# Held value products in the first attention, and an opening that loads tokens and weights in turn

## The chip, the cores and the metric

The kernel runs on one NeuronCore of one Trainium2 chip. The metric is the device time of one execution in microseconds (us). TensorE multiplies matrices, VectorE (DVE) and ScalarE (ACT) work element by element, GpSimd (POOL) does a few small powers, and the queue of SyncE (SP) issues all the DMA transfers. Each engine takes its instructions in the order in which they stand in its own stream.

## What is computed

The reference is two transformer blocks on one sequence of 512 tokens of width 1024, all in float32. The change touches the first block alone, whose first half is this:

```python
h = rms_norm(x, norm_pre)
proj = h @ w_in
(q_n, k_c, v_c, k_s, v_s, k_w, v_w, g_n, z_n, ...) = split(proj)
# 8 query heads of 64, 2 groups of keys and values; gates g_n per head and branch
o_a = compressed attention + selected attention + window attention, each gated
y_a = (o_a * silu(z_n)) @ w_nsa_o
```

With 512 tokens the selected branch and the window branch are both plain causal softmax attention, over keys k_s, k_w and values v_s, v_w. The compressed branch attends to 31 summaries of the keys and values. Behind it the block has a retention, two gates and an output projection; the second block has two feed-forward layers, a mixer with a second attention and a state-space part, and a cross attention.

## The kernel before, in words

Tokens lie in four tiles of 128 (t from 0 to 3). **Projections** multiply float32 numbers split in two float32r parts, a high and a low one, with three products each (high by high, low by high, high by low): `proj_T` (line 143, products at line 164) and `proj_X` (line 194, products at line 209). `wload` (line 102) loads a chunk of weights of 128x1024 by one DMA (line 99, three buffers `raw`), and `split` (lines 82 and 83) makes the high part on ACT and the low part on DVE, in two buffers each of `whi` and `wlo`. `proj_X` goes over the chunks of weights (four of them for a depth of 1024) and multiplies each with all four token tiles; only for the last `tail` chunks it goes token tile by token tile, so that a tile can be consumed when it is done.

**The opening** (lines 309 to 319) issues the DMA of token tile 0, of the constants `cst` (with the identity for transposes) and of the gain, then of the other three token tiles. Each tile is normalised (`prenorm_tile`, line 242: a sum of squares on ACT at line 249, the power on POOL at line 76, the scaling on DVE at line 251), turned by eight float32 transposes on TensorE (line 236) and split into `a_hi` and `a_lo`. The first projection (line 402, keys and values of 512 columns) then asks for its weights.

**The first attention** (`attention`, line 485) takes one token tile of queries (`qi`) at a time. It begins with the compressed branch: scores at line 495, a softmax on DVE and ACT, two transposes at line 510, and eight value products at line 516 into the bank `ob`. Then come eight steps, two branches times four pairs of heads. A step has float32r score products (line 536), the mask and minimum on DVE (line 539), the exponential on ACT (line 541), small factors on DVE (lines 542 to 544), the scaling of the two heads on DVE (line 546), float32 transposes of the probabilities on TensorE (line 553, one for each head and key tile), copies of these out of PSUM on ACT and DVE (lines 556 and 558), and float32 value products (line 561, one for each head and key tile, 64 columns of weights each, two records in the trace for one product). `qi` has qi+1 key tiles. When all is in `ob`, `gated` (line 565) multiplies it with `zn` on DVE.

The float32 products (transposes and values) and the float32r products (scores and projections) share TensorE. The order in the engine streams is not the program's order: a planner places, by its own estimate of times, the earliest instruction in program order that is ready. So scores of later steps and products of the projections that follow in the program (`zn`, then the rotated queries and keys of the retention, all at line 164) are placed wherever a step of the attention waits. The second attention, in the mixer, has a form of its own: `after` (line 88) adds a dependence, the transposes of a step (line 1055) wait for the last DVE operation of that step (line 1048), and the value products (line 991) of the step before are held back and follow those transposes.

Of the kernel before, what the change touches and what calls it, by code (L numbers as in the profile page):

```python
# [7 lines left out]
F32 = mybir.dt.float32  # L8
F32R = mybir.dt.float32r
AF = mybir.ActivationFunctionType  # L10
ALU = mybir.AluOpType
# [20 lines left out]
def block_kernel(ctx, tc, A, out, upto=99):  # L32
# [69 lines left out]
    def wload(src, k0, nk, c0, w, slot=None):  # L102
        raw, _ = wraw(src, k0, nk, c0, w)
        n = nk * w
        hi, lo = slot() if slot else (wp.tile([128, 1024], F32R, name="whi"), wp.tile([128, 1024], F32R, name="wlo"))
        split(hi[:, :n], lo[:, :n], raw[:, :n])
        return (hi[:, :n].rearrange("p (k c) -> p k c", k=nk), lo[:, :n].rearrange("p (k c) -> p k c", k=nk))
# [85 lines left out]

    def proj_X(src, c0, w, get, consume, K=8, nt=NT, tail=1, kp=2, korder=None, between=None, slots=()):

# [21 lines left out]
        slots = (None,) * (tail - len(slots)) + tuple(slots)  # L217
        last = [(ch, wload(src, ko[ch * kp], min(kp, K - ch * kp), c0, w, slots[ch - nch])) for ch in range(nch - tail, nch)]
        for t in range(nt):
# [81 lines left out]
    def first_block():  # L301
# [7 lines left out]
        x0 = xp.tile([128, NT, D], F32, name="x_in", tag="x")  # L309
        for t in range(NT):  # L310
            nc.sync.dma_start(x0[:, t], x2d[:, t])
            if t == 0:
                nc.sync.dma_start(cst, A["c_a"])
                g0 = gain("norm_pre")
            if t == 0:
                pair = new_act()
            if t == 0:
                hs = l1.tile([128, NT, D], F32, name="hs", tag="s3")
            prenorm_tile(x0[:, t], g0, pair, t, halved(hs[:, t]))
        get = act_get(pair)  # L320
        cb_t = cb.tile([128, B_ALL], F32, name="cb_t")
# [9 lines left out]
        bcast(A["b_nsa_gate"], 24, bg)  # L331
        w_in = A["w_in"]

# [67 lines left out]

        proj_X(w_in, 512, 512, get, ev_kv)
        proj_X(w_in, 1024, 280, get, ev_kw)
# [74 lines left out]

        ns = [0]

# [4 lines left out]
        def attention(qi):  # L485
            ob = op_.tile([128, 512], F32, name="ob").rearrange("p (a q) -> p a q", a=4)
            qsl = slice(qi * 128, (qi + 1) * 128)
# [18 lines left out]
            V.scalar_tensor_tensor(c8, c8, valid[:, qi:qi + 1], gv[:, 0], op0=ALU.mult, op1=ALU.mult)  # L506
            V.tensor_tensor(pc, pc, c8[:, :, None].to_broadcast([128, 8, 32]), op=ALU.mult)
            tp = tpp.tile([128, 4, 128], F32, name="tp")
            for g in range(2):
                PE.transpose(tp[:, g], pc[:, g * 4:(g + 1) * 4].rearrange("p a b -> p (a b)"), ident)  # L510
            pT = l2.tile([128, 2, 128], F32, name="pTc", bufs=1)
            V.tensor_copy(pT, tp[:, 0:2])
            for a in range(4):
                for e in range(2):
                    h = 2 * a + e
                    PE.matmul(ob[64 * e:64 * e + 64, a], vcD[:, h // 4, h % 4], pT[:, h // 4], start=(a == 0), stop=False,
                              skip_group_check=True)

            nk = qi + 1
            W = nk * 128  # L520
            for br in range(2):
                for a in range(4):
# [22 lines left out]
                    for e in range(2):  # L545
                        V.tensor_scalar(p[:, e, :W], p[:, e, :W], c2[:, e:e + 1], None, op0=ALU.mult)
                    tp = None
                    for e in range(2):
                        if e == 0 or nk > 2:
                            tp = tpp.tile([128, 4, 128], F32, name="tp") if (e if nk > 2 else a % 2) else bank((2,)).rearrange("p (j q) -> p j q", j=4)  # L550
                            o = 0
                        for j in range(nk):
                            PE.transpose(tp[:, o + j], p[:, e, j * 128:(j + 1) * 128], ident)  # L553
                        o += nk
                        if nk > 2:
                            (V.tensor_copy if e else ACT.copy)(pT[:, e, :nk], tp[:, :nk])
                    if nk <= 2:
                        (V.tensor_copy if a % 2 else ACT.copy)(pT[:, :, :nk], tp[:, :2 * nk].rearrange("p (e j) q -> p e j q", e=2))
                    for j in range(nk):
                        for e in range(2):  # L560
                            PE.matmul(ob[64 * e:64 * e + 64, a], vv[:, j, br, g * 64:(g + 1) * 64], pT[:, e, j], start=False,  # L561
                                      stop=(br == 1 and j == nk - 1), skip_group_check=True)
            return ob

        def gated(qi, ob):
            V.tensor_tensor(zn[:, :, qi * 128:(qi + 1) * 128], zn[:, :, qi * 128:(qi + 1) * 128], ob, op=ALU.mult)

# [4 lines left out]

        ob = attention(0)
        proj_T(w_in, 1304, 512, get, ev_zn, of=(0, 1))
        gated(0, ob)
        for qi in range(1, NT):
            gated(qi, attention(qi))

# [689 lines left out]
```

## Time and profile before

| | us |
|---|---|
| median of three runs | 1963.53 |
| lowest and highest of them | 1960.84, 1966.74 |
| the profiled execution, its own time | 1966.04 |
| its span in the trace | 1964.3 |
| TensorE busy in the span | 1907.7 |

The profile is of one execution. Its page gives busy time by engine, the chain of work that ended last, and groups of instructions by line. The trace behind it can be asked for the instructions in order of time (a timeline, in which neighbours of one kind are merged), for groups by line within a stretch, for the busy time of every engine in given stretches, and for waits (which engine waited before which line, for whom, how long and how often). A busy TensorE is an upper bound of its work, because the ends of products are modelled: the start of one product and the start of the next say more than their durations.

### The profile page before, as it was taken

What the parts mean: (1) busy time and instruction counts of PE and PEld (TensorE: products, weight loads), DVE (VectorE), ACT (ScalarE), POOL (GpSimd) and SP (SyncE); (2) the same over time, 40 slices, a digit from 0 to 9 for tenths busy, and PEclk for the clock granted to TensorE, in tenths of its full rate; (3) what the DMA queues carried; (4) which work ended last, traced back from release to release, by engine and by line L of the source; (5) the groups of instructions that cost most, each with busy time, mean ns of one, the idle gap of its engine ahead of it and who ended that gap; (6) DMA issues with size and microseconds to landing.
All of it is one profiled execution on the core that took longest, in us unless ns stands there. A gap on an engine that the chain in (4) does not pass through costs nothing.

```text
span 1964.3 us, 24168 instructions
## 1 busy us (share of the span) xinstructions
PE 1907.7 (97%) x9676; PEld 1555.6 (79%) x9676; DVE 1002.7 (51%) x1712; ACT 709.0 (36%) x1190; POOL 38.0 (2%) x66
## 2 busy tenths in 40 slices
PE   7999999999999999999999999989999999999998
PEld 5677788788878888888877777667788888888887
DVE  5578743824563333323668666785464553333223
ACT  4345433223242222223445433344353432323221
POOL 0000000100000000000000000000000000000000
PEclk9999999999999999999999999999999999999999
DMA  7411033232323333234231255542262322333332
GB/s 243 119 55 33 23 87 97 74 118 87 97 95 97 98 98 97 97 97 129 74 96 43 76 135 124 130 127 67 84 192 87 97 65 86 97 97 97 97 97 86
DMA packets 153560, 191.10 MB, mean 97 GB/s; under 512 B 9732, under 2 KB 111464, under 8 KB 153320
## 3 DMA queue, kind: packets, MB, share of 16 engines
q1 hardware_dynamic: 153448, 189.56, 32.1%
q8 instruction: 76, 1.25, 0.3%
q14 instruction: 36, 0.29, 0.0%
HBM read 174.85 MB, written 2.10 MB: 90 GB/s over the span
## 4 chain that ended last, share of the span: by engine, by line
PE 80%; DVE 10%; ACT 2%; DMA 1%; issue 1%; POOL 1%; SPq 0%; POOLq 0%; DVEq 0%; ACTq 0%
PE mm L164 40%; PE mm L209 27%; PE mm L187 3%; DVE E L1045 2%; PE ob L561 1%; POOL rp_r L76 1%; DVE x_sb L279 1%; DVE l L1048 1%; DVE h L251 1%; DVE wlo L83 1%; PE ob L902 1%; PE s L536 1%; PE s L1143 1%; DVE fg L272 1%; PE mm L553 1%
## 5 line engine op out<-in xcount | busy, mean ns | idle before, releaser
L83 DVE TENSOR_TENSOR wlo<-raw,whi 128x1024 fp32r<-128x1024 f32 (+1 forms) x276 | 336.1, 1218 | 681.4 <-ACT whi L82 676.0
L82 ACT ACTIVATE whi<-raw 128x1024 fp32r<-128x1024 f32 (+1 forms) x276 | 291.1, 1055 | 698.5 <-PE mm L164 298.5
L164 PE MATMUL mm<-a_hi,wlo 128*128 128x512 f32 x1120 | 439.7, 393 | 1.9 <-DVE wlo L83 1.9
L164 PE MATMUL mm<-a_hi,whi 128*128 128x512 f32 x1120 | 440.2, 393 | 0.0
L164 PE MATMUL mm<-a_lo,whi 128*128 128x512 f32 x1120 | 439.3, 392 | 0.0
L164 PEld LDWEIGHTS mm<-a_hi,wlo 128*128 128x128 f32 x1120 | 210.4, 188 | 45.8 <-DVE wlo L83 2.4
L164 PEld LDWEIGHTS mm<-a_hi,whi 128*128 128x128 f32 x1120 | 210.4, 188 | 43.4 <-issue 1.4
L164 PEld LDWEIGHTS mm<-a_lo,whi 128*128 128x128 f32 x1120 | 210.4, 188 | 43.2 <-issue 2.1
L209 PE MATMUL mm<-whi,a_hi 128*128 128x512 f32 (+1 forms) x400 | 156.9, 393 | 1.5 <-ACT whi L82 0.8
L209 PE MATMUL mm<-whi,a_lo 128*128 128x512 f32 (+1 forms) x400 | 156.9, 392 | 0.0
L209 PE MATMUL mm<-wlo,a_hi 128*128 128x512 f32 (+1 forms) x400 | 155.1, 390 | 0.0
L209 PE MATMUL mm<-whi,hid_hi 128*128 128x512 f32 x288 | 112.0, 389 | 0.0
L209 PE MATMUL mm<-whi,hid_lo 128*128 128x512 f32 x288 | 112.0, 389 | 0.0
L209 PE MATMUL mm<-wlo,hid_hi 128*128 128x512 f32 x288 | 112.0, 389 | 0.0
L209 PEld LDWEIGHTS mm<-whi,a_hi 128*128 128x128 f32 x400 | 75.7, 189 | 18.9 <-issue 2.7
L209 PEld LDWEIGHTS mm<-whi,a_lo 128*128 128x128 f32 x400 | 75.6, 189 | 16.0 <-issue 2.3
L209 PEld LDWEIGHTS mm<-wlo,a_hi 128*128 128x128 f32 x400 | 75.1, 188 | 14.7 <-issue 1.6
L76 POOL TENSOR_TENSOR rp_r<-rp_a,half 128x1 f32<-128x1 f32 (+1 forms) x58 | 35.9, 619 | 1896.3 <-DVE rp_a L74 1569.1
L209 PEld LDWEIGHTS mm<-whi,hid_lo 128*128 128x128 f32 x288 | 54.1, 188 | 11.3
L209 PEld LDWEIGHTS mm<-wlo,hid_hi 128*128 128x128 f32 x288 | 54.1, 188 | 11.3
L209 PEld LDWEIGHTS mm<-whi,hid_hi 128*128 128x128 f32 x288 | 54.1, 188 | 11.1
L1045 DVE TENSOR_TENSOR_SCAN E<-l,own 128x128 f32<-128x128 f32 (+2 forms) x64 | 49.6, 810 | 8.7 <-ACT l L1036 8.7
(446 smaller groups left out, 2825.7 us busy)
## 6 DMA issues: line engine op xcount, KB each, us to landing
raw<-in_w_in_dram SPq DMA_DIRECT2D x96, 512.0 KB, 3.7
raw<-in_ffn_w_gu_dram SPq DMA_DIRECT2D x88, 512.0 KB, 3.6
raw<-in_ffn_w_down_dram SPq DMA_DIRECT2D x44, 512.0 KB, 3.7
raw<-in_w_out_dram SPq DMA_DIRECT2D x24, 512.0 KB, 3.8
raw<-in_xa_wkv_dram SPq DMA_DIRECT2D x16, 512.0 KB, 3.8
raw<-in_w_ret_o_dram SPq DMA_DIRECT2D x8, 512.0 KB, 3.4
K<-kh SPq DMA_DIRECT2D x32, 128.0 KB, 2.4
K<-kl SPq DMA_DIRECT2D x32, 128.0 KB, 2.4
```

The lines of the kernel that those rows point to most:

```text
L76: POOL.tensor_tensor(r[:, :n], a[:, :n], half[:, :n], op=ALU.pow)
L82: ACT.activation(hi, src, AF.Copy)
L83: V.tensor_tensor(lo, src, hi.bitcast(F32), op=ALU.subtract)
L164: PE.matmul(o, a, b, start=(kc + k == 0 and n == 0 and si == 0), stop=(kc + k == K - 1 and n == 2), skip_group_check=True)
L187: PE.matmul(banks[g][j][:, t0 * 128:t1 * 128], a, b, start=(kc + k + n + si == 0), stop=(kc == 1 and k == 3 and n == 2), skip_group_check= ...
L209: PE.matmul(banks[t][:, :w], a, b, start=(kk == 0 and n == 0), stop=(kk == K - 1 and n == 2))
L251: V.scalar_tensor_tensor(h, src, r, g, op0=ALU.mult, op1=ALU.mult)
L272: V.tensor_tensor(fgt, bank, gpost[:, hf * 512:(hf + 1) * 512], op=ALU.mult)
L279: V.scalar_tensor_tensor(xs, fg[:, t if q == 0 else NT + t % 2], r, xs, op0=ALU.mult, op1=ALU.add)
L536: PE.matmul(sbs[e], qS[:, h, qsl], kk[:, br, g, :W], start=(n == 0 and (e == 0 or nk > 2)), stop=(n == 1), skip_group_check=True)
L553: PE.transpose(tp[:, o + j], p[:, e, j * 128:(j + 1) * 128], ident)
L1045: V.tensor_tensor_scan(E[:, rev], l[:, off + W - 1:(off - 1) if off else None:-1], own1[:, 511:(511 - W) if W < 512 else None:-1], 1.0, op ...
```

## The change

There are two parts. At the opening, each token tile's DMA and normalisation is followed at once by the load and split of one of the four weight chunks of the first projection; the third and fourth chunk get a buffer of their own (`spare`, in space that the queries use later). `proj_X` takes the four ready chunks with `tail=4`, so its loop goes token tile by token tile over all chunks. The gain is loaded before the constants.

```diff
-    def proj_X(src, c0, w, get, consume, K=8, nt=NT, tail=1, kp=2, korder=None, between=None, slots=()):
+    def proj_X(src, c0, w, get, consume, K=8, nt=NT, tail=1, kp=2, korder=None, between=None, slots=(), ready=None):
...
-        last = [(ch, wload(src, ko[ch * kp], min(kp, K - ch * kp), c0, w, slots[ch - nch])) for ch in range(nch - tail, nch)]
+        last = ready or [(ch, wload(src, ko[ch * kp], min(kp, K - ch * kp), c0, w, slots[ch - nch])) for ch in range(nch - tail, nch)]
...
-        for t in range(NT):
+        spare = l1.tile([128, 4, 1024], F32R, name="wsl", tag="s1")
+
+        kv_w = []
+        for t, slot in enumerate((None, None, lambda: (spare[:, 0], spare[:, 1]), lambda: (spare[:, 2], spare[:, 3]))):
             nc.sync.dma_start(x0[:, t], x2d[:, t])
             if t == 0:
+                g0 = gain("norm_pre")
                 nc.sync.dma_start(cst, A["c_a"])
-                g0 = gain("norm_pre")
...
             prenorm_tile(x0[:, t], g0, pair, t, halved(hs[:, t]))
+            kv_w.append((t, wload(w_in, 2 * t, 2, 512, 512, slot)))
...
-        proj_X(w_in, 512, 512, get, ev_kv)
+        proj_X(w_in, 512, 512, get, ev_kv, tail=4, ready=kv_w)
```

In the first attention the transposes of a step wait for the last scaling of that step on DVE, and the value products of the step before, held in a list, follow them. The value products of the compressed branch are held in the same way. At a change of `qi` the last value products wait for the compressed softmax of the next `qi`; the bank `ob` is taken after they are placed. The multiplication with `zn` moves into the last value products of a `qi`.

```diff
-            V.tensor_tensor(pc, pc, c8[:, :, None].to_broadcast([128, 8, 32]), op=ALU.mult)
+            last = V.tensor_tensor(pc, pc, c8[:, :, None].to_broadcast([128, 8, 32]), op=ALU.mult)
...
+            if held:
+                held.pop()(last)
+            ob = op_.tile([128, 512], F32, name="ob").rearrange("p (a q) -> p a q", a=4)
+
+            def compressed(*others):
...
+                        if h == 0:
+                            after(m, *others)
+            held.append(compressed)
...
+            def values(br, a, pT):
+                def f(*others):
+                    g = a // 2
+                    for j in range(nk):
+                        for e in range(2):
+                            m = PE.matmul(ob[64 * e:64 * e + 64, a], vv[:, j, br, g * 64:(g + 1) * 64], pT[:, e, j], start=False,
+                                          stop=(br == 1 and j == nk - 1), skip_group_check=True)
+                            if j + e == 0:
+                                after(m, *others)
+                    if br == 1 and a == 3:
+                        zq = zn[:, :, qi * 128:(qi + 1) * 128]
+                        V.tensor_tensor(zq, zq, ob, op=ALU.mult)
+                return f
...
-                        V.tensor_scalar(p[:, e, :W], p[:, e, :W], c2[:, e:e + 1], None, op0=ALU.mult)
+                        last = V.tensor_scalar(p[:, e, :W], p[:, e, :W], c2[:, e:e + 1], None, op0=ALU.mult)
...
-                            PE.transpose(tp[:, o + j], p[:, e, j * 128:(j + 1) * 128], ident)
+                            m = PE.transpose(tp[:, o + j], p[:, e, j * 128:(j + 1) * 128], ident)
+                            if e + j == 0:
+                                after(m, last)
...
-                    for j in range(nk):
-                        for e in range(2):
-                            PE.matmul(ob[64 * e:64 * e + 64, a], vv[:, j, br, g * 64:(g + 1) * 64], pT[:, e, j], start=False,
-                                      stop=(br == 1 and j == nk - 1), skip_group_check=True)
-            return ob
+                    held.pop()(last)
+                    held.append(values(br, a, pT))
...
-        ob = attention(0)
+        attention(0)
         proj_T(w_in, 1304, 512, get, ev_zn, of=(0, 1))
-        gated(0, ob)
         for qi in range(1, NT):
-            gated(qi, attention(qi))
+            attention(qi)
+        held.pop()()
```

## Rows read from the trace of the kernel before

**Rows 1.** The page: busy time by engine, with its share of the span and instructions.
```profile
PE 1907.7 (97%) x9676; PEld 1555.6 (79%) x9676; DVE 1002.7 (51%) x1712; ACT 709.0 (36%) x1190; POOL 38.0 (2%) x66
```

**Rows 2.** Stretches: length, busy PE, PEld, DVE, ACT, POOL, PEclk, DMA share, GB/s.
```profile
0.00:17.85 17.85, 5.05 (x21) 3.86 (x21) 7.48 (x16) 8.93 (x15) 1.99 (x8) 1.00 0.90 334
...
114.38:139.10 24.72, 23.01 (x157) 17.19 (x157) 18.88 (x94) 10.70 (x41) 0.00 (x0) 1.00 0.16 43
...
207.40:244.60 37.20, 36.98 (x277) 27.28 (x275) 29.60 (x84) 18.82 (x42) 0.00 (x0) 1.00 0.11 30
```

**Rows 3.** Timeline of TensorE in the last `qi`: start, length, engine, line, tiles, count.
```profile
219.19 0.40 PE L164 MATMUL mm<-a_hi,wlo 128*128 128x512 f32 x1
...
221.04 0.40 PE L164 MATMUL mm<-a_lo,whi 128*128 128x512 f32 x1
221.28 0.60 PE L553 MATMUL mm<-cst,p 128*128 128x128 f32 x4
221.72 0.60 PE L553 MATMUL tp<-cst,p 128*128 128x128 f32 x4
...
222.61 0.43 PE L561 MATMUL ob<-pT,vv 128*64 128x128 f32 x2
222.97 0.65 PE L553 MATMUL mm<-cst,p 128*128 128x128 f32 x4
```

**Rows 4.** TensorE's groups by line, 207.4 to 244.6 us: busy, mean ns, idle before.
```profile
L561 PE MATMUL ob<-pT,vv 128*64 128x128 f32 x128 | 11.7, 282 | 0.2
L164 PE MATMUL mm<-a_hi,whi 128*128 128x512 f32 x15 | 6.5, 431 | 0.0
...
L553 PE MATMUL mm<-cst,p 128*128 128x128 f32 x32 | 5.0, 279 | 0.0
...
L536 PE MATMUL s<-kAB,qS 128*128 128x512 f32 x14 | 4.9, 431 | 0.0
L536 PE MATMUL mm<-kAB,qS 128*128 128x512 f32 x8 | 2.8, 418 | 0.0
L516 PE MATMUL ob<-pTc,vcD 128*64 128x128 f32 x16 | 1.1, 279 | 0.0
```

**Rows 5.** Timeline of TensorE in the second attention, 1189 to 1194 us.
```profile
1189.91 0.55 PE L1055 MATMUL tp<-cst,l 128*128 128x128 f32 x3 [1.01 <-DVE l L1048]
1190.30 0.49 PE L1055 MATMUL mm<-cst,l 128*128 128x128 f32 x3
1190.72 1.09 PE L991 MATMUL ob<-aT,vv 128*64 128x128 f32 x16
1191.74 0.50 PE L164 MATMUL mm<-a_hi,wlo 128*128 128x512 f32 x1
...
1193.49 0.49 PE L1055 MATMUL tp<-cst,l 128*128 128x128 f32 x3
```

**Rows 6.** TensorE's longest wait over the whole span: total us, times, longest.
```profile
PE tp L1055 <- DVE l L1048: 10.5, 15, 1.3
```

**Rows 7.** Timeline of the opening, all engines, releasers in brackets.
```profile
7.97 1.28 DVE L251 SCALAR_TENSOR_TENSOR hs<-x_in,rp_r,gain 128x1024 f32<-128x1024 f32 x1 [2.25 <-DMA gain<-in_norm_pre_dram]
9.14 0.34 SPq L404 DMA_DIRECT2D cb_t<-in_c_b_dram  x1
17.83 1.23 DVE L83 TENSOR_TENSOR wlo<-raw,whi 128x1024 fp32r<-128x1024 f32 x1 [0.19 <-ACT whi L82]
17.85 0.80 PE L209 MATMUL mm<-whi,a_hi 128*128 128x512 f32 x1 [0.78 <-ACT whi L82]
18.87 0.63 PE L209 MATMUL mm<-whi,a_hi 128*128 128x512 f32 x1
19.30 0.63 PE L209 MATMUL mm<-whi,a_lo 128*128 128x512 f32 x1
20.95 0.40 PE L209 MATMUL mm<-whi,a_hi 128*128 128x512 f32 x1
25.64 0.69 DVE L83 TENSOR_TENSOR a_lo<-tp,a_hi 128x512 fp32r<-128x512 f32 x1 [1.13 <-ACT a_hi L82]
```

More of the change, by code (lines that the diff above doesn't have):

```diff
@@ L309, in first_block @@
         x0 = xp.tile([128, NT, D], F32, name="x_in", tag="x")
-        for t in range(NT):
+        w_in = A["w_in"]
+        pair = new_act()
+        hs = l1.tile([128, NT, D], F32, name="hs", tag="s3")
+        spare = l1.tile([128, 4, 1024], F32R, name="wsl", tag="s1")
+        kv_w = []
+        for t, slot in enumerate((None, None, lambda: (spare[:, 0], spare[:, 1]), lambda: (spare[:, 2], spare[:, 3]))):
             nc.sync.dma_start(x0[:, t], x2d[:, t])
             if t == 0:
+                g0 = gain("norm_pre")
                 nc.sync.dma_start(cst, A["c_a"])
-                g0 = gain("norm_pre")
[L315 to L318, printed above, removed]
             prenorm_tile(x0[:, t], g0, pair, t, halved(hs[:, t]))
+            kv_w.append((t, wload(w_in, 2 * t, 2, 512, 512, slot)))
         get = act_get(pair)
@@ L331, in first_block @@
         bcast(A["b_nsa_gate"], 24, bg)
-        w_in = A["w_in"]
         qS = l1.tile([128, 8, 512], F32R, name="qS", tag="s1")
@@ L476, in first_block @@
             V.tensor_copy(vcD[32 * r:32 * r + 32, :, r], po[32 * r:32 * r + 32, 64:192].rearrange("p (a b) -> p a b", a=2))
-        ns = [0]
+        ns, held = [0], []
         def sbank():
@@ L485, in attention @@
         def attention(qi):
-            ob = op_.tile([128, 512], F32, name="ob").rearrange("p (a q) -> p a q", a=4)
             qsl = slice(qi * 128, (qi + 1) * 128)
@@ L510, in attention @@
                 PE.transpose(tp[:, g], pc[:, g * 4:(g + 1) * 4].rearrange("p a b -> p (a b)"), ident)
-            pT = l2.tile([128, 2, 128], F32, name="pTc", bufs=1)
-            V.tensor_copy(pT, tp[:, 0:2])
-            for a in range(4):
-                for e in range(2):
-                    h = 2 * a + e
-                    PE.matmul(ob[64 * e:64 * e + 64, a], vcD[:, h // 4, h % 4], pT[:, h // 4], start=(a == 0), stop=False,
-                              skip_group_check=True)
+            pTc = l2.tile([128, 2, 128], F32, name="pTc", bufs=1)
+            V.tensor_copy(pTc, tp[:, 0:2])
+            if held:
+                held.pop()(last)
+            ob = op_.tile([128, 512], F32, name="ob").rearrange("p (a q) -> p a q", a=4)
+            def compressed(*others):
+                for a in range(4):
+                    for e in range(2):
+                        h = 2 * a + e
+                        m = PE.matmul(ob[64 * e:64 * e + 64, a], vcD[:, h // 4, h % 4], pTc[:, h // 4], start=(a == 0), stop=False,
+                                      skip_group_check=True)
+                        if h == 0:
+                            after(m, *others)
+            held.append(compressed)
             nk = qi + 1
             W = nk * 128
+            def values(br, a, pT):
+                def f(*others):
+                    g = a // 2
+                    for j in range(nk):
+                        for e in range(2):
+                            m = PE.matmul(ob[64 * e:64 * e + 64, a], vv[:, j, br, g * 64:(g + 1) * 64], pT[:, e, j], start=False,
[6 more added lines that the diff above has]
+                return f
             for br in range(2):
@@ L558, in attention @@
                         (V.tensor_copy if a % 2 else ACT.copy)(pT[:, :, :nk], tp[:, :2 * nk].rearrange("p (e j) q -> p e j q", e=2))
-                    for j in range(nk):
-                        for e in range(2):
-                            PE.matmul(ob[64 * e:64 * e + 64, a], vv[:, j, br, g * 64:(g + 1) * 64], pT[:, e, j], start=False,
-                                      stop=(br == 1 and j == nk - 1), skip_group_check=True)
-            return ob
-        def gated(qi, ob):
-            V.tensor_tensor(zn[:, :, qi * 128:(qi + 1) * 128], zn[:, :, qi * 128:(qi + 1) * 128], ob, op=ALU.mult)
+                    held.pop()(last)
+                    held.append(values(br, a, pT))
         def ev_zn(j, bank):
```

## The prediction

> **What bounds the kernel now.** I read the page first, then busy time by stretches, then TensorE's timeline where the change works. On the page TensorE is busy 97% of the span and no other engine over 51% [rows 1]: time that TensorE loses or gains in a stretch goes, as a rule, straight into the end. The stretches show two different places [rows 2]. In the first 17.85 us TensorE has 5.05 us of work, all transposes: here the data bind. In the attention it has no idle time to speak of (37.20 us long, 36.98 busy at the last `qi`), and DVE, 29.60 of 37.20, is the next in line. But "busy" there is not work. The reader should look at starts: eight steps from 219.19 to 221.04 give 0.231 us for a float32r product of 512 columns, and four transposes from 221.28 to 221.72 give 0.11 (0.109 over longer series) for a float32 product of 128 columns [rows 3]; value products run at the same pace, two records each. Then the stretch of the last `qi` can be added up [rows 4]: 64 value products, 64 transposes (32 into `mm`, as many into `tp`), 8 compressed value products and 2 compressed transposes are 138 x 0.109 = 15.0 us; 45 projection products (three groups of 15) and 22 score products are 67 x 0.231 = 15.5 us. That is 30.5 of 37.2 us; 6.7 us are lost though almost none of it is called idle. Where: after eight transposes comes one projection product, one value product (222.61), four transposes (222.97), and so on [rows 3]. The value products wait for copies of transposes made just before, and TensorE turns from float32 to float32r and back. I count 18 unbroken runs of float32 products in this stretch, so a break costs 6.7/18 = 0.37 us, waits included. In the stretch before I count 22 runs, in the first two 31 together.
>
> **The attention.** After the change a step's transposes are followed at once by the value products of the step before, whose copies were made a step ago. There are 32 steps and 4 compressed beginnings: 36 runs, 9 for each `qi`. No product, copy or DVE operation is added or taken away; only the order changes and one wait is added (on the second head's scaling, where the first head's transposes needed only the first). What a run of this form costs, the second attention shows, which has it already [rows 5]: from 1189.91 to 1193.49, 3.58 us, there are 14 float32 products (3, 3 and 16 records of 8) and 7 float32r ones, 14 x 0.109 + 7 x 0.231 = 3.14 us. So 0.43 us is lost per run, without a wait ahead of it. For the last `qi`: 6.7 - 9 x 0.43 = 2.8 us gained. `qi` 2 has more runs now and the same form: again 2.8. At the first two a run is of two to eight products and its copies are short, so I don't give 13 vanished runs the full 0.37 (that would be 4.8) nor nothing: what is plainly lost there is the idle 24.72 - 23.01 = 1.7 us of `qi` 0 [rows 2], and I take 1.5. Sum 7.1.
>
> Against that stand the new waits. Behind a transpose that waits stand, on TensorE's in-order stream, all products of scores and projections placed after it, and behind these the DVE and ACT work that feeds on them. Now TensorE's idle time before the transposes at the last `qi` is 0.0 [rows 4], so the planner's idea of when the scaling is done fits there; in the second attention the same kind of wait costs 10.5 us in 15 of 24 steps [rows 6]. I am nearer to the first, because the chain ahead (line 546) stays the same and is one DVE operation later, and charge 1 us. **Attention: -6 us**; bounds +8.7 (the second attention's waits on every run, below) and -13.7 (each run at 0.25 us, so 6.7 - 9 x 0.25 = 4.45 at each of the last two `qi`, and 4.8 at the first two). The held products cost a step's delay of `ob`, whose only reader is the product with `zn`, and that is not read before the retention's projections are through; the second buffer of `pT` covers the delay of the copies. If DVE, at 29.6 of 37.2 us, became the pace, TensorE would take projection products that are due next instead, and the gain stays.
>
> **The opening.** Moved, per token tile: one DMA on SP's queue, the sum of squares and two splits of `a` on ACT, one power on POOL, scaling and two `a_lo` on DVE, eight transposes; per weight chunk one DMA, one `whi` on ACT, one `wlo` on DVE. All exist before. New is the order on the queue: tile 0, gain, constants, chunk 0, tile 1, chunk 1 and so on. At 334 GB/s [rows 2] a 0.52 MB piece takes 1.6 us, so tile 1 comes 1.6 us later, tile 3 some 4.7 us later, and the gain, which released the first scaling at 7.97 [rows 7], up to 0.4 us earlier. Chunk 0 has 1.7 MB before and with it, some 5 us of transfer from the start at about 2 us: there at 7 to 9. Then the first products need the scaling (1.28), transposes, a split of `a` and one of `w`: about 11.5 instead of 17.85. TensorE can't be fed from there on: DVE must do four scalings (1.28), eight `a_lo` (0.69) and four `wlo` (1.23) [rows 7], 15.6 us, not before 7.5, so to 23 at the earliest (the last `a_lo` starts at 25.64 now). And early products are slow: those at 18.87 and 19.30 are 0.43 apart and 0.63 long, at 20.95 they are 0.40 long [rows 7], so TensorE was at 1.2 GHz until it had worked without a pause for about 3 us, and then at 2.4. Of the 6.3 us I let 2.8 go to starved and slow products: **opening -3.5 us**. Bounds: 0 (all of it given back) and -6.3. Tile by tile consumption moves the rotations and transposes of keys earlier; they are as many as before.
>
> The Trainium skill, "TensorE: Matmul & The Clock Gate", Part 1, says that the half clock is the default state and that only sustained activity lifts it, with idle gaps bringing it back. By the rows alone the slow stretch costs about what it does now; by that rule a TensorE fed in drips from 11.5 on could stay slow until the splits are done, which is the second rival below, with half of the opening's gain or all of it gone.
>
> **Sum.** -6 - 3.5 = -9.5 us. From the profiled execution's 1966.04 (span 1964.3) that is 1956.5; it stands 2.5 above the median of 1963.53, so on the median's scale **1954.0**. A measurement of this kernel can tell about 0.3%, 5.9 us, from no change.
>
> **Rivals.**
> 1. Only the opening pays: the runs are placed as told, but the waits for the scaling take what the breaks cost. Price 7 us over 36 runs, 0.2 us each. For it: the rows of the second attention. Against it: no idle time before transposes now. 1963.5 - 3.5 = 1960.
> 2. Only the attention pays: the first products start early at the half clock and with pauses, and the splits on DVE end when they do now. Or the large constant transfer that SP issues at 9.14 [rows 7], 1.9 MB or 5 us, goes ahead of the fourth weight chunk, which must wait for a free `raw` buffer (three of them for four chunks), and every token tile needs that chunk to be finished. For it: the chunk's wait is in the code. Against it: three chunks for four tiles are 72 products, 16.6 us of work. 1963.5 - 6 = 1957.5.
> 3. Slower: the transposes wait as in the second attention. 10.5 us over its 24 steps is 0.44 us a step [rows 6]; times 36 is 15.8, less 7.1 of breaks saved is +8.7, less the opening's 3.5 is +5.2: 1968.7. It decides from a mean new wait of (7.1 + 3.5)/36 = 0.29 us a run on. For it: same form, same planner. Against it: there the chain has a scan and a difference on DVE behind ACT, here the chain is one that the planner places without idle time.
> 4. The planner breaks the runs again with products that it finds ready in between, so the attention doesn't change: it does so in some steps of the second attention. That ends with rival 1, about 1960.
>
> **How the numbers follow.** Forecast 0.50, rival 1 with rival 4 0.22, rival 2 0.18, rival 3 0.10. The range has the forecast's bounds without their far ends (-20 and +5) and rivals 1, 2 and 4: 1945 to 1963. Faster by over 0.3% (under 1957.6): nearly all of the forecast and most of rival 2, 0.62. Within: rivals 1 and 4, the rest of rival 2 and of the forecast, 0.29. Slower by over 0.3%: the upper half of rival 3, and mishaps of its kind, 0.09.
>
> **What would show it.** Right: the first product of line 209 at about 11 to 13 us and the first projection's end 3 to 4 us earlier; some 36 to 45 float32 runs instead of 71, a value group of 2 x (qi+1) products straight behind the transposes; the stretch of the last `qi` some 3 us shorter at the same count of projection products; little idle time of TensorE before line 553's transposes. Wrong: idle time there of over 0.3 us a step; single projection products still standing between transposes and values; a long pause of TensorE before 25 us behind the fourth weight chunk; or a later stage that waits for a transfer and gives the gain back.

## The result and the profile after

Six runs of the changed kernel have a median of 1953.03 us (1951.14 to 1957.59), six of the kernel before on the same chip 1962.44 (1960.0 to 1966.74). The ratio is 0.9948, with a 95% interval of 0.9936 to 0.9959: 10 us (8 to 13) less, over the 0.3% that can be told. The profiled execution took 1957.59 us, the longest of the six; its span is 1955.8, 8.5 less than before.

Line numbers moved. In the changed kernel the attention's transposes are line 579, value products 538, scores 561, compressed value products 523, compressed transposes 512. `wsl` is the buffer of the third and fourth weight chunk.

The page's row of engines answers to [rows 1]:

```profile
PE 1903.7 (97%) x9676; PEld 1557.1 (80%) x9676; DVE 1003.9 (51%) x1712; ACT 708.7 (36%) x1190; POOL 38.3 (2%) x66
```

Same instructions, same shares. TensorE's busy time fell by 4.0 us, the span by 8.5. So over half of the gain is idle time that went, and the rest was called busy.

Where it came from is read by comparing the start of the same product in both traces. The first product of line 209 is 6.27 us earlier, the last of the first projection (the 96th) 0.02, the last of the second projection 1.63, the last of the third (the queries) 3.24, the first product of line 209 behind the attention 8.14. From there to the end it stays between 8.1 and 8.8, and the spans differ by 8.5. So 3.2 us come before the attention's stage, 4.9 in it, and next to nothing later.

Stretches of the changed kernel, with the columns of [rows 2]:

```profile
0.00:16.14 16.14, 5.66 (x20) 4.36 (x21) 7.71 (x13) 8.19 (x12) 1.31 (x6) 1.00 0.87 305
16.14:57.28 41.14, 40.29 (x229) 34.21 (x228) 23.49 (x70) 16.40 (x34) 3.30 (x6) 1.00 0.61 196
...
57.28:90.93 33.65, 32.33 (x160) 22.36 (x159) 18.51 (x51) 9.36 (x21) 0.00 (x0) 1.00 0.48 141
...
111.12:139.10 27.98, 26.25 (x152) 19.24 (x152) 19.01 (x94) 10.71 (x41) 0.00 (x0) 0.88 0.14 38
...
124.50:132.00 7.50, 7.50 (x28) 4.99 (x28) 3.65 (x22) 3.08 (x10) 0.00 (x0) 0.54 0.00 0
...
203.65:236.63 32.98, 32.98 (x284) 26.53 (x282) 29.93 (x84) 18.75 (x40) 0.00 (x0) 1.00 0.12 34
```

and the stretches of the kernel before that answer to its second and third:

```profile
17.85:58.91 41.06, 40.74 (x228) 34.96 (x228) 22.95 (x67) 15.87 (x32) 2.27 (x5) 1.00 0.57 172
58.91:94.17 35.26, 32.33 (x160) 22.27 (x159) 18.58 (x52) 9.43 (x21) 0.00 (x0) 1.00 0.45 135
```

**The opening.** 16.14 and 17.85 are the points from which TensorE works with hardly a pause. From there to the end of the second projection both kernels take the same time, 41.14 and 41.06 us. So of the 6.27 us at the first product only the 1.71 between these points count. The third projection then has 32.33 us of work in both and takes 33.65 instead of 35.26. The 1.6 us between them is one wait of TensorE for a transfer, which the profile of the kernel before has (58 to 98 us: total, times, longest) and that of the changed kernel has not:

```profile
PE ob L446 <- DMA w1t<-in_cmp_w_k_dram: 1.6, 1, 1.6
```

But it is not the change that took it away. A second profile of the changed kernel (e1 below) has it again, and one with the old opening (e3) shows no such wait:

```profile
PE ob L449 <- DMA w1t<-in_cmp_w_k_dram: 1.4, 1, 1.4
```

So it comes and goes between executions, and what the rows leave to the opening itself is the 1.6 us at the end of the second projection.

The timeline of the changed kernel's opening (start, length, engine, line, tiles, count, releaser) shows why the early products brought so little:

```profile
6.81 1.28 DVE L251 SCALAR_TENSOR_TENSOR hs<-x_in,rp_r,gain 128x1024 f32<-128x1024 f32 x1 [1.22 <-DMA gain<-in_norm_pre_dram]
...
10.94 0.38 SPq L99 DMA_DIRECT2D raw<-in_w_in_dram  x1
...
11.58 0.80 PE L209 MATMUL mm<-whi,a_hi 128*128 128x512 f32 x1 [1.47 <-ACT a_hi L82]
...
11.90 1.28 DVE L251 SCALAR_TENSOR_TENSOR hs<-x_in,rp_r,gain 128x1024 f32<-128x1024 f32 x1 [0.67 <-POOL rp_r L76]
...
13.11 0.68 DVE L83 TENSOR_TENSOR a_lo<-s,a_hi 128x512 fp32r<-128x512 f32 x1
13.24 1.12 PE L236 MATMUL s<-cst,hs 128*128 128x128 f32 x4 [0.86 <-DVE hs L251]
...
14.01 0.78 PE L209 MATMUL mm<-whi,a_lo 128*128 128x512 f32 x1
...
15.44 1.05 PE L236 MATMUL tp<-cst,hs 128*128 128x128 f32 x4
...
16.14 0.78 PE L209 MATMUL mm<-whi,a_lo 128*128 128x512 f32 x1
...
18.85 0.51 PE L209 MATMUL mm<-whi,a_lo 128*128 128x512 f32 x1
19.19 0.40 PE L209 MATMUL mm<-wlo,a_hi 128*128 128x512 f32 x1
```

Between 11.58 and 16.14 there are four products and the eight transposes of the next token tile. The second product needs `a_lo`, which DVE makes at 13.11, behind the next tile's scaling at 11.90; and it stands behind four of the transposes, which wait for that scaling. The fifth stands behind the other four. From 16.14 the starts are 0.43 us apart (0.58 the first), half pace, and 0.23 from 19.19 on.

**The attention.** The last `qi` answers to [rows 3]: eight transposes, sixteen records of values, and again.

```profile
231.72 0.60 PE L579 MATMUL mm<-cst,p 128*128 128x128 f32 x4
232.16 0.60 PE L579 MATMUL tp<-cst,p 128*128 128x128 f32 x4
232.69 1.09 PE L538 MATMUL ob<-pT,vv 128*64 128x128 f32 x16
233.71 0.66 PE L579 MATMUL mm<-cst,p 128*128 128x128 f32 x4
```

and TensorE's groups in the stretch from 203.65 to 236.63 us answer to [rows 4]:

```profile
L538 PE MATMUL ob<-pT,vv 128*64 128x128 f32 x140 | 9.4, 278 | 0.0
L164 PE MATMUL mm<-a_hi,wlo 128*128 128x512 f32 x14 | 5.5, 392 | 0.0
L164 PE MATMUL mm<-a_hi,whi 128*128 128x512 f32 x13 | 5.2, 401 | 0.0
L164 PE MATMUL mm<-a_lo,whi 128*128 128x512 f32 x13 | 5.1, 391 | 0.0
L579 PE MATMUL mm<-cst,p 128*128 128x128 f32 x32 | 5.0, 279 | 0.0
L579 PE MATMUL tp<-cst,p 128*128 128x128 f32 x32 | 4.8, 272 | 0.0
L561 PE MATMUL s<-kAB,qS 128*128 128x512 f32 x14 | 4.4, 410 | 0.0
L561 PE MATMUL mm<-kAB,qS 128*128 128x512 f32 x8 | 3.0, 434 | 0.0
L523 PE MATMUL ob<-pTc,vcD 128*64 128x128 f32 x16 | 1.1, 279 | 0.0
L512 PE MATMUL tp<-cst,pc 128*128 128x128 f32 x2 | 0.4, 270 | 0.0
```

Added up as in the prediction: 70 + 8 value products and 66 transposes are 144 x 0.109 = 15.7 us, 40 + 22 float32r products 62 x 0.231 = 14.3; 30.0 of 32.98 us, so 3.0 are lost, where 6.7 were.

The same sum over the whole attention, from the 48th product of line 164 to the last value product (184 products of line 164 in both; narrower score products at the pace of their own series, 0.11 to 0.17 us), is called **lost time** below. A `qi` here runs from the last value product of the one before to its own last, so the last one of the kernel before loses 7.3 us, and not the 6.7 of the prediction's stretch. Before it is 4.7, 3.1, 7.4 and 7.3 us at the four `qi`, 22.4 together; after, 8.5, 3.1, 3.1 and 3.0, 17.7. The 8.5 hold a disturbance: in the stretch 124.50:132.00 above the granted clock is 0.54, so for 6.8 us of it TensorE was granted 1.2 GHz. Another execution (first experiment) has not got it, and loses 5.5 there and 14.6 in all.

### The profile page after: what moved, and what is told of

The parts are those of the page before. It is cut to its first block, busy times and chain, and to the rows that moved or that the text cites. A ratio compares the mean times of both kernels' runs of the same rounds, so it can differ in the third digit from the quotient of the medians.

```text
span 1955.8 us, 24155 instructions
## 1 busy us (share of the span) xinstructions
PE 1903.7 (97%) x9676; PEld 1557.1 (80%) x9676; DVE 1003.9 (51%) x1712; ACT 708.7 (36%) x1190; POOL 38.3 (2%) x66
## 4 chain that ended last, share of the span: by engine, by line
PE 81%; DVE 11%; ACT 1%; POOL 1%; issue 1%; DMA 1%; POOLq 0%; DVEq 0%; SPq 0%; ACTq 0%
PE mm L164 41%; PE mm L209 27%; PE mm L187 3%; DVE E L1067 2%; POOL rp_r L76 1%; DVE x_sb L279 1%; DVE l L1070 1%; PE ob L538 1%; DVE h L251 1%; DVE wlo L83 1%; PE s L561 1%; PE ob L924 1%; PE s L1165 1%; DVE fg L272 1%; PE mm L579 1%
## 5 line engine op out<-in xcount | busy, mean ns | idle before, releaser
L209 PE MATMUL mm<-whi,a_hi 128*128 128x512 f32 (+1 forms) x384 | 150.6, 393 | 2.2 <-ACT a_hi L82 2.2
L209 PE MATMUL mm<-whi,a_lo 128*128 128x512 f32 (+1 forms) x384 | 151.1, 393 | 0.0
L209 PE MATMUL mm<-wlo,a_hi 128*128 128x512 f32 (+1 forms) x384 | 149.5, 391 | 0.0
L209 PEld LDWEIGHTS mm<-wlo,a_hi 128*128 128x128 f32 x384 | 72.5, 189 | 14.3 <-issue 1.6
## 6 DMA issues: line engine op xcount, KB each, us to landing
K<-kh SPq DMA_DIRECT2D x32, 128.0 KB, 2.4
K<-kl SPq DMA_DIRECT2D x32, 128.0 KB, 2.3
```

What stands on the lines that cost most here:

```text
L209: PE.matmul(banks[t][:, :w], a, b, start=(kk == 0 and n == 0), stop=(kk == K - 1 and n == 2))
```

## The experiments

All ratios are to the kernel before on the same chip, with their 95% interval. The expectations name theories by letters. Two decide about the attention. By the prediction's own, a turn of TensorE between float32 and float32r costs, so the count of float32 runs sets the time (D). By its rival the place of the value products sets it: they no longer wait for copies made just before, and they stand in one piece (C). E is about the opening, that the order within the first projection does not matter. Beside the lost time I count two things in each trace, over the same stretch: unbroken runs of float32 products, and unbroken **groups of value products** (the compressed ones not counted). This table is worked out from the traces; "stage" goes from the first product of line 164 to the first of line 209 behind the attention.

| kernel | stage us | lost time us | float32 runs | value groups |
|---|---|---|---|---|
| before | 159.74 | 22.4 | 70 | 45 |
| changed, undisturbed (e1) | 151.87 | 14.6 | 31 | 31 |
| e4, held, no waits | 161.90 | 24.5 | 72 | 49 |
| e5, values apart | 157.53 | 20.4 | 66 | 42 |
| e7, held from `qi` 1 | 151.12 | 13.9 | 36 | 30 |
| e8, pairs of steps | 149.74 | 12.3 | 25 | 24 |
| e9, zero product between | 159.60 | 14.8 | 59 | 32 |
| e10, zero product behind | 159.48 | 15.6 | 37 | 32 |

In the last two the added products count as work in the lost time, so that only what they cost beyond their own 0.231 us shows.

**1. The changed kernel again.** No edit.

> The changed kernel once more, for a second profile. Theory A (the stretch of half clock at 125 to 132 us of the first profile belongs to the chance of one execution): no half-clock stretch in the attention of this profile, and the stretch of qi 0 takes some 24.5 us instead of 28; ratio 0.995. Theory B (it belongs to the new order, whose qi 0 leaves TensorE too little to do): it is there again, at the same place.

Ratio 0.9956 (0.9942 to 0.997), 1955.9 us. Its stage (columns of [rows 2]), at full clock, PEclk 1.00:

```profile
96.17:248.04 151.87, 150.09 (x1066) 119.88 (x1064) 124.25 (x415) 79.28 (x198) 0.00 (x0) 1.00 0.15 43
```

7.9 us less than before's 159.74, where the first profile of the changed kernel had 154.85 with the half clock in it.

**2. The opening alone.** The attention is put back.

```diff
-                            m = PE.transpose(tp[:, o + j], p[:, e, j * 128:(j + 1) * 128], ident)
-                            if e + j == 0:
-                                after(m, last)
+                            PE.transpose(tp[:, o + j], p[:, e, j * 128:(j + 1) * 128], ident)
...
-                    held.pop()(last)
-                    held.append(values(br, a, pT))
```

> Only the opening of the change, the attention as before. Theory A (the two parts add): 3.3 us less than before, ratio 0.9983, the first projection ends no earlier than before and the gain appears after it, in the next two projections. Rival (the opening alone is given back at the first projection's end): ratio 1.000.

Ratio 0.9989 (0.9981 to 0.9998): 2.2 us less, between 0.4 and 3.7. Its stage is 159.77 us, lost time and counts as before: the opening does nothing to the attention.

**3. The attention alone.** The opening is put back.

```diff
-            kv_w.append((t, wload(w_in, 2 * t, 2, 512, 512, slot)))
...
-        proj_X(w_in, 512, 512, get, ev_kv, tail=4, ready=kv_w)
+        proj_X(w_in, 512, 512, get, ev_kv)
```

> Only the attention of the change, the opening as before. Theory A (parts add): 6 to 8 us less than before, ratio 0.996 to 0.997, qi 0 and 1 no shorter, qi 2 and 3 some 4 us shorter each. Rival (the attention gains all of the 9.4 us and the opening nothing): ratio 0.995.

Ratio 0.9971 (0.9962 to 0.998): 5.7 us less, between 3.9 and 7.5. The parts add: 2.2 + 5.7 = 7.9, where the whole gave 8.6 here and 10.2 in its own comparison. Its stage is 153.33 us, and it too has a stretch at 1.2 GHz at the first `qi`, 3.4 us from 128.0, with a lost time of 16.1.

**4. Held, but free to be placed.** The values stay held for a step, but no transpose and no value product waits for the scaling.

```diff
-                            if j + e == 0:
-                                after(m, *others)
...
-                            if e + j == 0:
-                                after(m, last)
```

> The changed kernel without the added dependences: value products are still issued a step later in program order, but neither they nor the transposes wait for the last scaling, so the planner may place them as soon as they are ready. Theory C (a break costs what the copies' wait costs: who holds the values back has no wait and needs no joined runs): as fast as the changed kernel, ratio 0.995, with about as many float32 runs as before. Theory D (a break costs the turn between float32 and float32r, only joined runs save it): the attention gains under 2 us, ratio 0.998, about 70 runs.

Ratio 0.9995 (0.9986 to 1.0004): nothing is left of the attention's gain, nor of the opening's. The planner placed the values singly behind their own copies again, so the two theories weren't told apart: runs and value groups both went back. What it shows is that holding does nothing unless the waits pin the order.

**5. Values apart from the transposes.** The held values wait for the first of the small DVE operations behind the exponentials instead of the last scaling, and stand ahead of the transposes, so that the two make two runs.

```diff
-                    V.tensor_scalar(c2, c2, TINY, None, op0=ALU.max)
+                    first = V.tensor_scalar(c2, c2, TINY, None, op0=ALU.max)
+                    held.pop()(first)
...
-                    held.pop()(last)
```

> The changed kernel, but the value products of the step before wait for the first small DVE operation after the exponentials, about 1 us ahead of the scaling, and are placed there: a run of their own, a step later than before the change, so without the wait for their copies; the transposes stand in a second run. Theory D (the turn between float32 and float32r costs by itself, some 0.25 us a break): about 65 runs, 30 to 35 more than with the change, and 6 to 9 us of the attention's 7.7 us gain are gone; ratio 0.999. Theory C (the wait for the copies was the loss): the gain stays but for 1 us, ratio 0.9955.

Ratio 0.9973 (0.996 to 0.9985), 1959.14 us, between the two theories. TensorE's timeline at the last `qi` shows what the planner made of it (here the transposes are line 580):

```profile
217.80 0.60 PE L580 MATMUL tp<-cst,p 128*128 128x128 f32 x4
218.16 0.48 PE L164 MATMUL mm<-a_hi,wlo 128*128 128x512 f32 x1
218.70 0.43 PE L538 MATMUL ob<-pT,vv 128*64 128x128 f32 x2
219.06 0.65 PE L580 MATMUL mm<-cst,p 128*128 128x128 f32 x4
219.65 1.09 PE L538 MATMUL ob<-pT,vv 128*64 128x128 f32 x14
220.66 0.66 PE L580 MATMUL tp<-cst,p 128*128 128x128 f32 x4
```

The first value product, which alone was told what to wait for, stands by itself, and the other seven are placed when their copies are there. The single one takes 0.36 us from its start to the next (219.06 - 218.70), 0.25 over its pace, and the seven 1.01 (220.66 - 219.65), again 0.25 over theirs; the waits of the weight loads name the copies, as they do before (total, times, longest; first this kernel, then the kernel before):

```profile
PEld ob L538 <- ACT pT L585: 3.7, 10, 0.5
```

```profile
PEld ob L561 <- ACT pT L556: 4.0, 11, 0.5
```

The changed kernel has no such wait. So this kernel, too, moved both counts together.

**6 and 7. A turn added, the values untouched.** In each step one float32r product of 512 columns with zero weights goes into the bank `ob` between the transposes and the values (e9), or behind the values (e10). The sums don't change. The edit of e10 leaves out the last step of each `qi`: it adds 28 products, not the 31 of its expectation.

```diff
+        zer = n1.tile([128, 128], F32R, name="zer")
...
+                    z = PE.matmul(obf, zer, kA[:, 0, 0, :], start=False, stop=False, skip_group_check=True)
+                    after(z, *others)
```

> The changed kernel with one more float32r product of 512 columns in each step, zero weights added into ob, placed between the step's transposes and the held values: 32 of them, 7.4 us of work at 0.231 us. It makes a second run of float32 products in each step without a wait for any copy. Theory D (a turn costs 0.25 to 0.36 us whatever is waited for): the attention is 15 to 19 us longer than the changed kernel's, 7.4 of work and 8 to 11 of turns. Theory C (only the copies' wait cost): 7.4 us longer.

> The same zero products, 31 of them, placed behind the held values, where most runs end in any case. Theory D: 7.2 us of work, and a turn only where two steps are joined in one run now (about 10 places, 3 us): some 10 us longer than the changed kernel, 6 to 8 us shorter than with the zero product in between. Theory C: 7.2 us longer, the same as in between.

Ratios 0.997 (0.996 to 0.9981) and 0.9977 (0.9966 to 0.9987). First e9, then e10, TensorE's timeline at the last `qi`:

```profile
213.95 0.60 PE L586 MATMUL mm<-cst,p 128*128 128x128 f32 x4
214.38 0.60 PE L586 MATMUL tp<-cst,p 128*128 128x128 f32 x4
214.74 0.48 PE L541 MATMUL ob<-kAB,zer 128*128 128x512 f32 x1
215.15 1.09 PE L545 MATMUL ob<-pT,vv 128*64 128x128 f32 x16
216.17 0.66 PE L586 MATMUL mm<-cst,p 128*128 128x128 f32 x4
```

```profile
213.85 0.61 PE L586 MATMUL mm<-cst,p 128*128 128x128 f32 x4
214.29 0.60 PE L586 MATMUL tp<-cst,p 128*128 128x128 f32 x4
214.82 1.09 PE L543 MATMUL ob<-pT,vv 128*64 128x128 f32 x16
215.85 0.51 PE L548 MATMUL ob<-kAB,zer 128*128 128x512 f32 x1
216.19 0.60 PE L586 MATMUL mm<-cst,p 128*128 128x128 f32 x4
```

A step of e9, transposes to transposes, is 216.17 - 213.95 = 2.22 us; in the changed kernel it was 233.71 - 231.72 = 1.99 without the product. The difference is 0.23, the product's own pace: the turn to float32r and back is free there. In e10 it is 0.35. Over the stage e9 takes 7.7 us more than the undisturbed changed kernel, for 32 products, which are 32 x 0.231 = 7.4. It has 28 more float32 runs (59 to 31): 0.3/28 = 0.01 us a turn. By the prediction's price, 0.37 to 0.43, 28 more would have cost 10 to 12 us beyond the work. That theory (D) falls. e10 has 22 runs fewer than e9 and four products fewer (0.9 us), and its stage is only 0.1 us shorter: beyond its products it loses 0.8 us more (15.6 to 14.8), where D had 6 to 8 less in time.

**8. The order of the first projection.** The first three chunks are multiplied chunk by chunk, only the last one tile by tile.

```diff
+        if ready:
+            for ch, hl in last[:-1]:
+                for t in range(nt):
+                    mms(t, ch, hl)
+            last = last[-1:]
```

> The changed kernel with its early loads, but the first projection goes chunk by chunk over all token tiles for three chunks, and token tile by token tile only for the last. Theory E (TensorE is without pause from 16 us on, so the order within the projection only moves transposes from after its end to before it): same time as the changed kernel, ratio 0.995, the end of the first projection 1 to 2 us earlier and the end of the second the same. Rival F (the order by token tiles is what feeds TensorE at 11 to 16 us): 1 to 3 us longer than the changed kernel.

Ratio 0.9951 (0.9937 to 0.9965), 1953.61 us. Two stretches, to the end of the first projection and to the end of the second:

```profile
0.00:40.82 40.82, 30.36 (x133) 23.95 (x134) 21.44 (x48) 17.53 (x27) 4.66 (x11) 1.00 0.80 273
40.82:56.41 15.59, 15.45 (x116) 14.47 (x116) 8.91 (x35) 6.74 (x19) 0.71 (x1) 1.00 0.37 120
```

The first projection ends 2.7 us earlier than in the changed kernel, at 40.82, with 133 records in it where that has 146; the second ends at 56.41, 0.9 us earlier than there and 0.55 earlier than in e1 (56.96). Most of what came out of the first came back in the second. E holds in the time; the shift was larger than the 1 to 2 us expected: tile by tile, transposes of keys are done inside the first projection, chunk by chunk behind it.

**9 and 10. Fewer changes at the short `qi`.** e7 has the old form at `qi` 0; e8 lets two steps share one run at `qi` 0 and 1.

```diff
-                            if e + j == 0:
+                            if qi and e + j == 0:
...
+                    if qi or (br == 1 and a == 3):
```

```diff
+                    steps.append((br, a, p, pT))
+                    if nk > 2 or a % 2:
+                        for br_, a_, p_, pT_ in steps:
+                            transposes(a_, p_, pT_, last)
+                        while held:
+                            held.pop(0)(last)
```

> The changed kernel with qi 0 in the old form (no waits, its values at once). Theory G (the new form leaves TensorE too little to do at qi 0, so that its clock falls there in most executions): no half-clock stretch at 115 to 140 us, and 1 to 3 us less than the changed kernel, ratio 0.9935 to 0.9945. Theory A (the half-clock stretches fall where they like): ratio as the changed kernel's, 0.995.

> The changed kernel, and at qi 0 and 1 two steps share one run: the transposes of both wait for the second one's scaling, then come the held values of the two steps before. Theory D (a break costs 0.25 to 0.4 us): some 8 runs fewer, 2 to 3 us less, ratio 0.9935. Rival (the wait for the second step's scaling is longer than the breaks are dear): idle time of TensorE before the transposes of qi 0 and 1 of over 3 us, ratio 0.996 or more.

Ratios 0.9944 (0.9931 to 0.9956), 1952.62 us, and 0.9939 (0.9926 to 0.9951), 1952.28 us. e7 loses 4.7 us at `qi` 0, as the kernel before does, where e1 loses 5.5: the new form brings nothing at the first `qi`. e8 has the shortest stage, 2.1 us under e1's:

```profile
95.22:244.96 149.74, 148.59 (x1066) 120.78 (x1064) 121.66 (x415) 79.74 (x198) 0.00 (x0) 1.00 0.15 42
```

In the runs neither can be told from the changed kernel, whose interval overlaps. The 2 to 3 us that D gave for e8 came in the trace, but here too the value groups fell with the runs (24 for 31, and 25 for 31), so it does not speak for D against e9.

**11. Pairs of steps and chunk by chunk together.** Both edits above.

> Pairs of steps at qi 0 and 1, and the first projection chunk by chunk. If the attention's gain of the pairs (2 us in the trace) holds, ratio 0.993 to 0.9945, at or below the changed kernel's; if it was chance, 0.995.

Ratio 0.9939 (0.9924 to 0.9954), 1953.13 us, with a stage of 149.72: no better than the pairs alone.

**12. The changed kernel a third time.** No edit, one run.

> The changed kernel a third time for its clock alone. Theory A: no half-clock stretch at 120 to 135 us, as in the second profile. Theory B: one there, as in the first.

It took 1956.85 us, and the granted clock was again at half for 6.8 us, from 124.1.

## Why the prediction was right, and where its reasons were not

**The time.** 1954.0 was forecast; 1953.03 came, with a ratio that leaves 8 to 13 us. The forecast's case, both parts paying, is the one that came. That the number lies so near is in part luck: the opening was forecast 1 to 2 us too high, and the attention's halves were wrong in opposite directions. Timed alone, the two parts give 7.9 us for the 9.5.

**What a break costs.** This step failed, although its sum came out. The prediction took the lost 6.7 us of the last `qi`, divided by 18 runs and called 0.37 us the price of a break, "waits included", with the turn between float32 and float32r as one of two causes; it then carried over 0.43 us a run from the second attention. The turn costs 0.01 us (e9). The unit was wrong: kernels with 59 runs (e9) and 31 (e1) lose the same 14.8 and 14.6 us. What orders all eight rows of the table is the number of value groups: 24, 30 to 32, 42, 45 and 49 groups go with 12.3, 13.9 to 15.6, 20.4, 22.4 and 24.5 us. From 31 to 45 groups that is 7.8/14 = 0.56 us a group, and e5 against e9 says the same (66 and 59 runs, but 42 and 32 groups, and 20.4 against 14.8 us).

That is a slope and not yet a cause. The starts of the single products, summed over the same stretch in the kernel before and in e1, say where the 7.8 us lie. First, the ends of a group. A group with an even number of value products takes 0.15 us more than its products at 0.109 each, up to the start of what follows it (eight from 232.69 to 233.71 in the changed kernel: 1.02 for 0.87). One with an odd number takes 0.25 us more than its products (the one and the seven of e5; in the kernel before the one at 222.61 in [rows 3]). In even groups the records start two by two, 0.007 us apart; in an odd one the two of one product stand alone. The kernel before has 28 odd groups and 17 even ones, e1 has 31 even ones: 9.6 us against 4.7. Second, the start of a group. Behind a transpose, with its copies there, its first product starts 0.09 us behind pace (30 of the 31 groups of e1); in the kernel before it starts up to 0.4 us behind. That is 6.8 us against 2.9, and some 2.9 of the 6.8 (6.8 - 43 x 0.09) are waits (of the 4.0 us that the weight loads wait for copies, a part passes beside products that still run). Third, against these 8.8 us stand 2.8: a float32r product right behind a transpose starts 0.08 us ahead of the transpose's pace, 41 times in the kernel before and 4 times in e1. The last 1.8 are spread over other places.

So most of the gain is that value groups are no longer split, and split into odd pieces at that; the waits for copies made just before, which theory C put first, are the smaller part. Why the ends of a group cost this is not shown. It seems to go with the 64 columns of weights: two value groups of the kernel before follow compressed products, which have 64 too, and start on pace.

**The attention's sum.** At the last two `qi` 2.8 us each were forecast; the undisturbed execution gained 4.3 each (7.4 and 7.3 to 3.1 and 3.0): the price of 0.43 left 9 x 0.43 = 3.9 us in the last `qi`, and 3.0 were left, of 7.3 instead of 6.7. At the first two 1.5 was forecast and -0.8 came: the idle time of `qi` 0, on which the 1.5 rested, stayed, 27.98 - 26.25 = 1.73 us in the changed kernel's stretch (24.72 - 23.01 before), and the time lost there rose. The two errors offset each other: 7.8 of lost time (22.4 - 14.6) against 7.1. The new waits were put at 1 us. In the waits of TensorE from 109 to 240 us (total, times, longest) one stands out, at the first `qi`:

```profile
PE tp L579 <- DVE c L567: 1.0, 1, 1.0
```

It is the only new one of any size; the 0.5 us next to it was there before. Timed, the part gave 5.7 us (3.9 to 7.5) for the -6.

**The opening.** The first product came at 11.58 for the "about 11.5". The step that failed is "I let 2.8 go": of the 6.27 us, 4.6 were gone at 16.14, in four products and eight transposes at half pace and in the wait for the next tile's scaling, and the end of the first projection, forecast 3 to 4 us earlier, did not move. The rows give 1.6 us for the forecast 3.5. The other 1.6 by which the queries come earlier are the wait for `w1t`, and that is chance: e1 has the new opening and waits 1.4 us there, e3 has the old one and does not. Timed, the part gave 2.2 (0.4 to 3.7).

The rule cited from the Trainium skill, "TensorE: Matmul & The Clock Gate", Part 1, agrees with the rows as far as they go: the four separated products did not lift the pace, and it rose only in the stretch worked without a pause from 16.14. From there on the slow products cost no more than before, since both kernels take the same time from that point to the end of the second projection.

**The rivals.** The first (only the opening pays) falls with e3, the second (only the attention pays) with e2, whose interval ends just short of 1. The second's transfer did not happen: SP issued the fourth weight chunk at 10.94, and the 1.9 MB of constants at 19.78 (its place in the queue is behind it now); at 334 GB/s they would have been 5.7 us and not 5. The third falls with the rows on waits. The fourth is what e4 shows: without the waits the planner does break the runs again.

**The signs.** Forecast were 36 to 45 runs, and 31 came, because the values of one step and the transposes of the next join where two steps are ready together (the sixteen records at 232.69 are followed at once by line 579). The last `qi` lost 3.7 us less, for the 3 forecast.

## What to carry to other kernels

Before a lost time is priced by counting turns, insert one product of known pace at each turn and look: here 28 more turns cost nothing, and a kernel with a few more turns but split value groups lost 5.6 us more. Then read from the starts what the ends of a group cost: here a group of value products is worth keeping whole, and even in number. Products that read a copy made just before are worth holding back for one step, but only with an added wait that pins the order, and where a step is long enough to cover it; at the shortest tiles the same wait cost 0.8 us more than it brought in the traces (5.5 to 4.7), too little to be seen in the runs. An opening's first product says little; the point from which the bounding engine works without a pause is what moves the end.

## What had not been expected of the hardware

Stretches at half the granted clock (1.2 GHz), of 3.4 or 6.8 us, appear in thirteen of the fourteen profiles, up to three in each (one in the last 5 us of every kernel not counted), although TensorE is busy 97% of the span. One place is common: eleven have one that begins between 1341 and 1356 us. Other places differ between executions of the same kernel. At the first `qi` it appears behind a pause: in all five profiles of kernels whose first `qi` is that of the changed kernel (the changed kernel three times, e3, e6) TensorE stands still for 1.03 us ahead of a transpose, in the first until 124.44, and in three of them the granted clock falls 0.5 to 1.4 us later (at 124.9 in the changed kernel, 128.0 in e3, 124.1 in e12); in the nine other profiles, where no pause there is longer than 0.91 (e10), it never does. It costs about 3 us where it is 6.8 long (17.7 against 14.6 of lost time), and may be part of why the changed kernel's runs spread over 6 us; the kernel before, whose profile has none there, spreads as far. That the pause sets it off is likely, not shown: e7 and e8, whose longest pauses there are 0.66 and 0.35, have one profile each, and the pause of 1.03 in e1 and e6 was followed by none.

The PEclk of 1.00 of the first stretch is no reading. In the trace the record of the granted clock begins with a rise to full at 19.1 us (20.9 in the kernel before), and what lies ahead of it is counted as full. The starts show the half pace there: 0.43 us apart from 16.72 to 18.85, and 0.23 from 19.19 on, where the record begins.
